# Where the scan's gate weights are split, who writes its reciprocals, and what its query parts are queued behind

## The chip, the cores and the metric

The kernel runs on one core of one Trainium2 chip. The metric is device time in microseconds (us) of one execution. The engines in the profile are PE (TensorE: matmuls, with PEld for its weight loads), DVE (VectorE), ACT (ScalarE), POOL (GpSimd) and SP (SyncE, which here only issues DMAs). Each engine works through its own queue in order.

## The reference

The program is one block of a latent generator with batch 1, 2048 latent tokens, 256 context tokens, width 1024 and depth 1: a gated linear recurrence (HGRN2, 8 heads of 128, both directions), then a gated convolutional feed-forward, both with RMS norm, shift, scale and gate. What matters here is the recurrence of one head and direction, in chunks:

```python
q, zf_fwd, zf_bwd, v, g = jnp.split(h @ w_in, 5, axis=-1)
f = lb[d] + (1.0 - lb[d]) * jax.nn.sigmoid(zf)      # forget gates, k = 1 - f
b = jnp.cumsum(jnp.log(f), axis=3)                  # within a chunk
scores = jnp.where(mask, (q * jnp.exp(b - b_ref)) @ (k * jnp.exp(b_ref - b)).T, 0.0)
kv = (k * jnp.exp(b_last - b)).T @ v                # a chunk's addition to the state
s = decay[..., None] * s + kv                       # from chunk to chunk
o = scores @ v + (q * jnp.exp(b)) @ s_start
```

Context tokens come first: the latent scans start from the states that they end in. The result of both directions is normalized per head, gated, multiplied by the output weights and added to the residual stream.

## The kernel before

All matmuls work on fp32 operands that are split in two parts (`split`, L79 to L82: ACT writes the high part at L80, DVE the rest at L81) and take three products each.

**The early stage** (`early`, L253 on) loads and normalizes the tokens and multiplies them by the weights of v, of the output gates and of q, by a scheme with seven products per block (`FACTORS`: B11, B21, T2, T1, T3, B22, T4). It goes once over the second half of the tokens (g = 1), then, from `turn_over` on, over the first half (g = 0), 84 products of four steps, each step three matmuls and one tick of a clock. Things beside the products are put on an agenda by tick (`at`). The generator `rest` is such a thing: `ada_rest` (L716) sums four rows of the modulation from 32 loads of `w_ada`, and `weights_rest` (L749) takes the two forget-gate weight matrices of each of the 8 heads, loads them raw (L757), splits them and stores both parts in DRAM (`w_d`, L766). Both work in one tile, `spare`, with the tag `cxt`: `weights_rest` uses two of its four rows for raw matrices and two for the result. 54 steps of `rest` are put on the agenda, five or six ticks apart; what is left of them is run out at the last T2 product of g = 0. Behind it the factor B12 is loaded again (`load_factor`, L782) into a tile with the same tag `cxt`, split, and put into the place that T2 held.

**The scan** (`mixer_scan`, L921) loads the split context tokens into a tile with that tag too (L1357) and goes over two groups of tokens (g = 0, 1) and over 8 heads in each. `head` (L1360) does, in group 0, the context's gates and states, and then for two units of four token tiles: `gate` (two projections of 48 matmuls' worth of work, L967 to L969, then sigmoid and bounds on ACT, L991 and L993) and `unit`. `weight` (L1344) loads the split forget-gate weights of the next head from `w_d`, or, for output gates, the raw ones through a buffer with two tiles (L1352).

`unit` calls `factors` (L1002), which scans the gates on DVE into prefix products `S` (L1011), forms `ke` from their differences, and lets GpSimd form the products of chunk totals (`TB`, `TX`, L1025 on). DVE takes the reciprocals of the 32 totals (`rt`, L1045), and GpSimd copies 15 of them into `d2` (L1046 and L1047), the second operand of the suffix scans (`suffix`, L1057). `rest` forms the query parts `qp` and `qi` and the key parts `km`, `kd` and part of `ke`. `unit_steps` has the matmuls behind it: `scores` (transposes L1100, scores L1144, mask on DVE L1161, sum `at` L1162), `stepped(p)` (products kv L1175, states on DVE L1178, copy `sk` on ACT L1181), and `outputs(p)` (L1196, L1199). The parts of a unit are put on the agenda at given ticks behind its gates, so that they fall among the gate matmuls of the next unit. A scheduler builds each engine's queue from the order in which instructions are traced and from when their inputs are ready by its own model; `tc.issue_after(i)` makes it put instructions behind `i` on that engine. `tied` (L1223) does so with the last entry of `made_last`, which `rest` and `scores` append to; it is used for the output weights that are scaled in the second group (L1243, L1249).

## Time and profile before

| what | us |
|---|---|
| median of 3 runs (2805.26 to 2810.89) | 2807.38 |
| profiled execution | 2804.56 |
| its span, first to last instruction | 2802.6 |
| early stage, to the last of its matmuls | 0 to 559.8 |
| scan | 612 to 1308 |
| output projection, up projection, down projection | 1308 to 2802 |

The span is shorter than the execution by 2.0 us, which lie around the instructions. Busy time is a union of an engine's instructions. A timeline row is: start, duration, engine, line, operation, output <- input, and in brackets how long the engine stood idle before it and what released it. A row of waits is: who waited, for whom, us in total, times, longest. SPq is SP's queue; its rows are issues of DMAs, not their transfers.

### The profile page before, as it was taken

What the parts mean: (1) busy time and instruction counts of PE and PEld (TensorE: products, weight loads), DVE (VectorE), ACT (ScalarE), POOL (GpSimd) and SP (SyncE); (2) the same over time, 40 slices, a digit from 0 to 9 for tenths busy, and PEclk for the clock granted to TensorE, in tenths of its full rate; (3) what the DMA queues carried; (4) which work ended last, traced back from release to release, by engine and by line L of the source; (5) the groups of instructions that cost most, each with busy time, mean ns of one, the idle gap of its engine ahead of it and who ended that gap; (6) DMA issues with size and microseconds to landing.
All of it is one profiled execution on the core that took longest, in us unless ns stands there. A gap on an engine that the chain in (4) does not pass through costs nothing.

```text
span 2802.6 us, 42181 instructions
## 1 busy us (share of the span) xinstructions
PE 2669.8 (95%) x15800; PEld 2219.7 (79%) x15800; DVE 2086.5 (74%) x2921; ACT 1191.1 (42%) x2051; POOL 610.4 (22%) x998
## 2 busy tenths in 40 slices
PE   7999999929999999999999999999999999999999
PEld 4788787828888777777888888888888888888887
DVE  4866876527777768786988888877878777577887
ACT  4744534412333222233666444444444444333444
POOL 1000333202222121121111443333444332000001
PEclk9999999969999999999999999999999999999999
DMA  8755766853343745445888522226322223888653
GB/s 325 278 194 203 244 211 204 288 218 114 93 132 119 247 134 192 151 130 191 288 300 324 209 91 90 88 70 237 134 89 91 91 72 113 293 294 282 208 191 128
DMA packets 260219, 514.90 MB, mean 184 GB/s; under 512 B 28448, under 2 KB 141488, under 8 KB 249392
## 3 DMA queue, kind: packets, MB, share of 16 engines
q1 hardware_dynamic: 255296, 502.98, 52.9%
q10 hardware_dynamic: 4720, 9.24, 0.9%
q8 instruction: 124, 2.03, 0.3%
q14 instruction: 79, 0.65, 0.1%
HBM read 352.48 MB, written 159.66 MB: 183 GB/s over the span
## 4 chain that ended last, share of the span: by engine, by line
PE 53%; DVE 3%; issue 1%; DMA 1%; ACT 1%; POOL 0%; POOLq 0%; DVEq 0%; ACTq 0%; SPq 0%
PE y L2096 5%; PE y L2095 5%; PE y L2097 5%; PE zc L1494 3%; PE zc L1496 3%; PE zc L1497 3%; PE zd L1497 3%; PE za L1497 3%; PE zd L1496 3%; PE za L1496 3%; PE zd L1494 3%; PE za L1494 3%; PE y L1598 2%; PE y L1600 2%; PE y L1599 2%; PE zb L1497 1%
## 5 line engine op out<-in xcount | busy, mean ns | idle before, releaser
L80 ACT ACTIVATE w<-raw 128x512 fp32r<-128x512 f32 (+1 forms) x270 | 169.2, 632 | 207.8 <-PE zd L1497 75.3
L81 DVE TENSOR_TENSOR w<-raw,w 128x512 fp32r<-128x512 f32 (+1 forms) x270 | 211.7, 788 | 50.8 <-ACT w L80 48.4
L2096 PE MATMUL y<-w,mh 128*128 128x512 f32 x600 | 233.5, 389 | 0.1
L2097 PE MATMUL y<-w,ml 128*128 128x512 f32 x600 | 233.4, 389 | 0.0
L2095 PE MATMUL y<-w,mh 128*128 128x512 f32 x600 | 233.2, 389 | 0.0
L81 DVE TENSOR_TENSOR w<-s,w 128x512 fp32r<-128x512 f32 x195 | 177.7, 915 | 71.4 <-ACT w L80 69.9
L80 ACT ACTIVATE w<-s 128x512 fp32r<-128x512 f32 x195 | 121.7, 630 | 199.6 <-POOL s L220 79.6
L1011 DVE TENSOR_TENSOR_SCAN S<-F,d 128x528 f32<-128x528 f32 (+1 forms) x80 | 91.4, 1143 | 103.1 <-ACT F L993 103.1
L76 POOL TENSOR_TENSOR rs<-rs,mhalf 128x1 f32<-128x1 f32 (+3 forms) x53 | 55.9, 1057 | 451.5 <-DVE rs L75 451.5
L967 PE MATMUL z<-tok,w 128*128 128x512 f32 x352 | 149.6, 425 | 0.0
L969 PE MATMUL z<-tok,w 128*128 128x512 f32 x352 | 141.5, 402 | 0.0
L968 PE MATMUL z<-tok,w 128*128 128x512 f32 x352 | 140.8, 400 | 0.0
L1494 PE MATMUL zc<-rT,w 128*128 128x512 f32 x352 | 137.1, 389 | 1.7 <-DMA rT<-rhs1T 1.7
L1496 PE MATMUL zc<-rT,w 128*128 128x512 f32 x352 | 137.0, 389 | 0.0
L1497 PE MATMUL zc<-rT,w 128*128 128x512 f32 x352 | 136.9, 389 | 0.0
L219 POOL TENSOR_TENSOR s<-raw 128x512 f32<-128x512 f32 x54 | 93.3, 1728 | 199.2 <-DMA raw<-in_w_up_dram 128.0
L2096 PEld LDWEIGHTS y<-w,mh 128*128 128x128 f32 x600 | 112.6, 188 | 23.7 <-DVE w L81 0.6
L2095 PEld LDWEIGHTS y<-w,mh 128*128 128x128 f32 x600 | 112.6, 188 | 23.7 <-ACT w L80 0.3
L2097 PEld LDWEIGHTS y<-w,ml 128*128 128x128 f32 x600 | 112.6, 188 | 23.5
L1496 PE MATMUL za<-rB,w 128*128 128x512 f32 x336 | 130.7, 389 | 0.0
L1497 PE MATMUL za<-rB,w 128*128 128x512 f32 x336 | 130.7, 389 | 0.0
L1494 PE MATMUL za<-rB,w 128*128 128x512 f32 x336 | 130.7, 389 | 0.0
(470 smaller groups left out, 7766.1 us busy)
## 6 DMA issues: line engine op xcount, KB each, us to landing
raw<-in_w_up_dram SPq DMA_DIRECT2D x88, 512.0 KB, 3.5
w<-w SPq DMA_DIRECT2D x32, 1024.0 KB, 8.2
raw<-in_w_in_dram SPq DMA_DIRECT2D x59, 512.0 KB, 4.6
lr<-m SPq DMA_DIRECT2D x49, 512.0 KB, 4.7
m<-r SPq DMA_DIRECT2D x66, 256.0 KB, 3.4
spare<-in_w_ada_dram SPq DMA_DIRECT2D x32, 512.0 KB, 4.8
w<-spare SPq DMA_DIRECT2D x16, 1024.0 KB, 4.9
kq<-stash SPq DMA_DIRECT2D x15, 1024.0 KB, 7.3
```

The source lines that it names most:

```text
L80: i = act.activation(h, src, AF.Copy)
L81: j = dve.tensor_tensor(l, src, h.bitcast(F32), OP.subtract)
L219: eng.tensor_tensor(s1, a21, a22, OP.add)
L967: pe.matmul(z, w[:, 0, k], h, start=k == 0, stop=False, skip_group_check=True)
L968: pe.matmul(z, w[:, 0, k], l, start=False, stop=False, skip_group_check=True)
L969: pe.matmul(z, w[:, 1, k], h, start=False, stop=k == KT - 1, skip_group_check=True)
L1494: pe.matmul(o, w[:, 0, k], r[:, :, 0, k], start=start and k == 0, stop=False, skip_group_check=True)
L1496: pe.matmul(o, w[:, 0, k], r[:, :, 1, k], start=False, stop=False, skip_group_check=True)
L1497: i = pe.matmul(o, w[:, 1, k], r[:, :, 0, k], start=False, stop=k == 3, skip_group_check=True)
L2095: pe.matmul(z, lh, rh, start=start, stop=False, skip_group_check=True)
L2096: pe.matmul(z, lh, rl, start=False, stop=False, skip_group_check=True)
L2097: pe.matmul(z, ll, rh, start=False, stop=stop, skip_group_check=True)
```

## The change

It has three parts. The forget-gate weights are no longer split by the early stage: `weights_rest` is gone, `rest` is `ada_rest` alone with 37 steps 7 ticks apart, and in the scan's first group `weight` loads the raw matrix, splits it and stores it to `w_d` for the second group. The reciprocals are written by DVE straight to where they are read: those of the suffix scans into `d2` (with one more chunk in it, for the scan's start value), the others into a smaller `rt`; the two copies on GpSimd are gone. And `rest` of a unit is tied behind the first two states of the unit before it: `made_last` is now appended to by `stepped(0)` alone. The last part of a unit moves from tick 30 to 31.

```diff
-        def weights_rest():
...
-            for n, (h, ty) in enumerate(todo):
-                load(n + 1)
-                w = hl.bitcast(F32R)
-                split(w[:, 0], w[:, 1], ring[:, n % 2])
-                sp.dma_start(w_d[h][ty - 1], hl.rearrange("p i n -> p (i n)"))
-                yield
...
-        rest = all_rest()
+        rest = ada_rest()
...
-                for m in range(54):
-                    at(clock[0] + 16 + 5 * m + m // 4, lambda: next(rest, None))
+                for m in range(37):
+                    at(clock[0] + 16 + 7 * m, lambda: next(rest, None))
...
-        d2 = fix.tile([128, 2, NS, SEG], F32, name="d2")
+        d2 = fix.tile([128, 2, NS + 1, SEG], F32, name="d2")
...
+            def strided(x, dist):
+                return bass.AP(tensor=x.tensor, offset=x.offset,
+                               ap=[list(x.ap[0]), [dist * SEG, 2], [2 * SEG, NS // 2]])
+
+            if u is not None:
+                dve.reciprocal(strided(d2[:, 0, 2, 0], NS), strided(S[:, 0, 1, 32], NS - 1))
+                rt = gp.tile([128, 2, NS // 2], F32, name="rt", tag="rt", bufs=2)
+                dve.reciprocal(rt, strided(S[:, 0, 0, 32], NS + 1))
...
-            rt = mid("rt", (2, NS))
-            dve.reciprocal(rt, S[:, :, :, 32])
-            pool.tensor_copy(d2[:, 0, 2:NS:2, 0], rt[:, 0, 1:NS - 1:2])
-            pool.tensor_copy(d2[:, 1, 1:NS:2, 0], rt[:, 1, 0:NS:2])
...
-                made_last.append(dve.tensor_tensor(halves(ke), halves(ke), halves(rt),
-                                                   OP.mult).ins)
+                c = ke[:, 0, 0, 0]
+                kh = bass.AP(tensor=c.tensor, offset=c.offset,
+                             ap=[list(c.ap[0]), [(NS + 1) * 32, 2], [64, NS // 2], [1, 32]])
+                scaled(kh, kh, rt)
...
-                made_last.append(dve.tensor_tensor(at_, AB[:, 0], AB[:, 1], OP.add).ins)
+                dve.tensor_tensor(at_, AB[:, 0], AB[:, 1], OP.add)
...
+                    moved = dve.scalar_tensor_tensor(st[s + 1], st[s], sd[:, 1, s:s + 1], kv[:, 1, i],
+                                                     OP.mult, OP.add).ins
+                if p == 0:
+                    made_last.append(moved)
...
-                if ty < 3:
+                if g and ty < 3:
                     sp.dma_start(flat, w_d[h][ty - 1])
                 else:
                     raw = rawp.tile([128, D], F32, name="raw", tag="raw")
                     sp.dma_start(raw, a["w_in"][h, ty])
                     split(w[:, 0], w[:, 1], raw.rearrange("p (k n) -> p k n", k=KT))
+                    if ty < 3:
+                        sp.dma_start(w_d[h][ty - 1], flat)
...
-                m, *parts = factors(h, u, t0[u], q, values(v_d[h][n]))
-                for f, dt in zip((*parts, *unit_steps(h, t0[u], m)), after):
+                m, suffix, rest = factors(h, u, t0[u], q, values(v_d[h][n]))
+                behind = (lambda: tied(rest)) if made_last else rest
+                for f, dt in zip((suffix, behind, *unit_steps(h, t0[u], m)), after):
                     at(clock[0] + dt, f)
```

## The prediction, made before the changed kernel was built or run

> **What bounds the kernel now.** I read the page first, for which engine the span is made of, then a table of stretches, then TensorE's own waits, then the timeline at the two places where it waits.

> ```profile
> span 2802.6 us, 42181 instructions
> PE   7999999929999999999999999999999999999999
> ...
> 450.00:559.50 109.50, 106.81 (x474) 86.74 (x472) 65.79 (x85) 47.89 (x76) 32.18 (x33) 1.00 0.74 253
> 559.50:612.00 52.50, 0.31 (x2) 0.00 (x0) 10.19 (x12) 7.66 (x11) 2.19 (x6) 0.53 0.79 296
> 612.00:634.00 22.00, 21.87 (x115) 19.67 (x116) 6.14 (x11) 6.76 (x11) 2.83 (x9) 0.88 0.02 7
> 634.00:948.00 314.00, 305.35 (x3047) 265.01 (x3046) 235.89 (x350) 94.78 (x187) 73.48 (x259) 1.00 0.43 133
> 948.00:1227.00 279.00, 257.93 (x2600) 218.05 (x2603) 208.90 (x291) 76.29 (x143) 50.52 (x197) 0.96 0.52 164
> 1227.00:1308.00 81.00, 75.22 (x766) 63.41 (x754) 60.18 (x97) 31.76 (x72) 13.16 (x45) 0.98 0.39 120
> ```

> The columns behind a stretch are its length, busy time of PE, PEld, DVE, ACT and POOL, granted clock, DMA share and GB/s. TensorE fills the span but for one slice, the ninth, and that slice is the hole 559.5 to 612.0 between the early products and the scan. In the scan's first group of heads (634 to 948) PE is idle 8.7 us in 314, in its second (948 to 1227) 21.1 us in 279, and there the granted clock is 0.96 too. DVE is at 75% in both. So time comes from holes in PE's queue, and no other engine is a bound of its own.

> PE's waits, for 450 to 559, 558.9 to 612.6, 634 to 948 and 948 to 1227:

> ```profile
> PE za L517 <- ACT u L546: 1.5, 2, 1.0
> ...
> 612.13 0.55 PE L967 MATMUL z<-cxt,w 128*128 128x256 f32 x1 [52.32 <-DMA cxt<-cxt]
> ...
> PE kv L1175 <- ACT sk L1181: 4.3, 7, 0.6
> PE o L1199 <- DVE at L1162: 2.9, 7, 1.6
> PE o L1196 <- DVE states L1178: 1.5, 7, 0.3
> ...
> PE kv L1175 <- ACT sk L1181: 10.6, 14, 1.1
> PE o L1196 <- DVE states L1178: 10.5, 14, 1.0
> ```

> **Part 1, the weights that leave the early stage.** What ended last in the hole, on SP, ACT, DVE and PE:

> ```profile
> 584.13 0.32 SPq L766 DMA_DIRECT2D w<-spare  x1
> 591.45 0.32 SPq L766 DMA_DIRECT2D w<-spare  x1
> 595.39 0.57 SPq L782 DMA_DIRECT2D fraw<-part  x1
> 604.03 0.33 SPq L1357 DMA_DIRECT2D cxt<-cxt  x1
> ...
> 589.11 1.06 ACT L80 ACTIVATE spare<-spare 128x1024 fp32r<-128x1024 f32 x1 [6.26 <-DMA w<-spare]
> 600.85 2.19 ACT L80 ACTIVATE tok<-fraw 128x512 fp32r<-128x512 f32 x4 [10.68 <-DMA fraw<-part]
> ...
> 590.20 1.22 DVE L81 TENSOR_TENSOR spare<-spare 128x1024 fp32r<-128x1024 f32 x1 [6.09 <-ACT spare L80]
> ...
> 559.42 0.39 PE L520 MATMUL zc<-rT,w 128*128 128x512 f32 x1
> ```

> The 16 weight matrices go through one output buffer: ACT stands until the previous store has landed, so one costs 7.3 us (584.13 to 591.45), and the chain of 16 outruns the products by 32 us. The tile is then needed twice more: for factor B12 (load at 595.39, in at 600.85, split until 604.03) and for the context tokens (load at 604.03, first matmul at 612.13). That is 3.9 us from the last store to the load, 5.5, 3.2 and 8.1 us.

> Removed from the early stage: 16 loads, 16 ACT (1.06 us), 16 DVE (1.22 us), 16 stores. Then the tile is free when the 37 steps of the ada sums are through, due at tick 16 + 7 x 36 = 268 of 336 from the turn-over. A tick is three matmuls, and 474 matmuls in 109.5 us are 0.231 us each, so the tile comes free about 68 x 0.69 = 47 us before 559.5, near 513. B12's load lands near 519. Its splits must wait for the end of the last T2 product, whose place B12 takes: 8 products of 12 matmuls, 22 us, before the end, 537. With 3.2 us of splitting and 8.1 us of load the context tokens are in near 549, 10 us before PE asks for them. The first scan weights now need raw loads and splits first:

> ```profile
> 525.75 0.38 SPq L1352 DMA_DIRECT2D raw<-in_w_in_dram  x1
> ...
> 542.19 0.33 SPq L1352 DMA_DIRECT2D raw<-in_w_in_dram  x1
> ```

> These two loads are for gate weights of the last head, used after 1227: SP sends a load as soon as its buffer is free, and both raw buffers are free by 542. The new loads take those slots, so two splits (2 x 1.22 us on DVE) fit ahead of 559.5. I take 1 us for what is left of the hole: **52.3 - 1 = 51.3 us** saved. The hole also leaves the clock low: 0.88 over 22 us is **2.6 us**, gone with it. Early PE waits for ACT's u, which stands behind the split that waits for its store, 1.5 us in two, go as well.

> In the scan's first group the same 16 splits are added, less 16 loads of 1 MB, and 16 stores and 16 raw loads more on SP. DVE gets 16 x 1.22 = 19.5 us in 314 us (75% to 81%), ACT 17 us on 30%. Behind a split on ACT stand the gates' sigmoids, behind it on DVE the scans, and PE waits for both; behind a store on SP stand loads of q and v. Bounds: 0 if they fall in idle time, 16 x (1.06 + 1.22) = 36 us if each holds PE for its whole length. I take the near end, because a quarter of DVE's time and two thirds of ACT's are idle there and PE has three gate banks, but book only half of what this group could gain (below).

> **Part 2, reciprocals and the order behind the states.** One unit of the second group, DVE, then PE:

> ```profile
> 968.84 0.35 DVE L1045 RECIPROCAL rt<-S 128x32 f32<-128x32 f32 x1
> 970.67 1.32 DVE L1057 TENSOR_TENSOR_SCAN S<-F,rt,d 128x528 f32<-128x528 f32 x1 [1.48 <-POOL d L1046]
> 973.05 1.29 DVE L1161 COPY_PREDICATED AB<-mbf,sc 128x1024 f32<-128x1024 uint32 x1
> 974.22 0.69 DVE L1063 TENSOR_TENSOR qp<-q,S 128x512 f32<-128x512 f32 x1
> 974.82 0.69 DVE L1162 TENSOR_TENSOR at<-AB 128x512 f32<-128x512 f32 x1
> 975.42 0.69 DVE L1064 TENSOR_TENSOR qp<-q,S 128x512 f32<-128x512 f32 x1
> 976.02 0.35 DVE L1178 SCALAR_TENSOR_TENSOR states<-Sf,sd,kv 128x128 f32<-128x128 f32 x1
> 977.42 0.35 DVE L1178 SCALAR_TENSOR_TENSOR states<-states,sd,kv 128x128 f32<-128x128 f32 x1
> ...
> 975.35 0.38 PE L1196 MATMUL o<-Sf,qi 128*128 128x128 f32 x2
> 976.42 0.49 PE L1196 MATMUL o<-states,qi 128*128 128x128 f32 x2 [0.37 <-DVE states L1178]
> 978.24 1.16 PE L1175 MATMUL kv<-v,kt 128*128 128x128 f32 x8 [1.10 <-ACT sk L1181]
> ```

> The suffix scan waits 1.48 us for GpSimd's copies of the reciprocals. With VectorE writing them itself nothing is left between: the suffix scans start 1.48 us sooner, less the second reciprocal. The trace has none of 16 elements; the nearest row is the 32-element one, 0.35 us, so two cost 0 to 0.35 us more than one; I take 0.2 and gain 1.3 us. Then the query parts: ahead of the second state stand qp twice (0.6 us apart each) and qi, which fills 976.3 to 977.4, 1.1 us: 2.3 us that the tie moves behind it. The second state then ends near 977.8 - 1.3 - 2.3 = 974.2 (its two states, 0.35 us each, back to back), ACT's copy at 974.6, before PE reaches its first output matmul at 975.35. Both waits of the unit go, with 0.7 us to spare. The tie adds a wait to the query parts; behind them on DVE stand km, kd and the next prefix scan, and PE's next transposes wait for kd. But states now end 3.6 us sooner, so the moved 2.3 us end sooner than they did.

> The second group's PE waits are 10.6 + 10.5 = 21.1 us in 14 units. Idle time counts from a matmul's modelled end, and one lasts 0.39 us (the row at 559.42) where they follow each other every 0.231, so each wait hides 0.16 us of lost overlap more: 28 x 0.16 = 4.5 us, together **26 us**. The clock:

> ```profile
> 1014.00:1020.00 6.00, 4.53 (x19) 3.80 (x19) 6.00 (x11) 1.36 (x3) 1.20 (x2) 0.73 0.71 173
> 1093.00:1099.00 6.00, 4.47 (x27) 3.68 (x26) 6.00 (x11) 1.96 (x4) 0.00 (x0) 1.00 0.39 134
> ```

> 0.96 over 279 us is 11.2 us. The 6 us with 1.5 us of idle PE at 1014 run at 0.73; the 6 us with the same idle at 1093 at full clock. I take it that the low clock comes from the idle time, in some of the units, and goes with it: **11 us**; the other end is 0.

> [...]

> First group: 4.3 + 2.9 + 1.5 = 8.7 us in 21 waits, 12 us with the lost overlap. Half of it, because of the splits: **6 us**. The last head and all behind the scan I leave as they are.

> **Sum:** 51.3 + 2.6 + 1.5 + 26 + 11 + 6 = 98.4 us. The profiled execution took 2804.6 us (2.0 around its span of 2802.6) and would take 2706.2; the median of the runs is 2.8 us above it, so **2709 us**. This case alone goes from 2694 (the hole's last 1 us, the other 6 of the first group, 5.8 of PE idle and 1.6 of clock in the last head) to 2718.

> **Rivals.**

> A, the chain to the context tokens is late: SP takes its queue in order, and the last store of the products is this:

> ```profile
> 562.19 0.51 SPq L529 DMA_DIRECT2D q<-out  x1
> ```

> If the context load goes behind it, it lands at 562.7 + 8.1 = 570.8, 11 us of hole; if B12's load and splits go there as well, 16.8 us and more. 10 to 16 us lost and some clock: 2722. For it: four early stores hold SP in turn. Against: loads were sent ahead of such stores in the rows above.

> B, another step of DVE takes the states' place, or the query parts aren't what held them: part 2 gives nothing in PE time, 26 + 11 + 6 = 43 us, 2752; half of it 2730. Against: a spare of 0.7 us and DVE at 75%.

> [...]

> D, the splits hold PE in the first group: up to 36 + 6 us, 2751; half 2730.

> E, slower than before. ACT takes its queue in order, and each split stands at its head until its raw transfer is in, as in the row at 589.11. If PE pays the early stage's whole 7.3 us cycle for each of 16, that is 117 us, and the first group's 6 aren't won: 2709 + 6 + 117 = 2832. It decides from 5.8 us a split on ((98.4 - 6) / 16). Against it: two raw buffers and loads a head ahead; PE has three gate banks. [...]

> **Chances.** Forecast 0.62, A 0.13, B 0.09, C 0.08, D 0.05, E 0.03. The range is 2691 (the near end, 2694, less the 2.8 us between runs) to 2736 (A, C and the halves of B and D are in; E and the ends of B and D are out). Faster than before by over 0.2% (5.6 us, about what a measurement of this kernel can tell from no change) is all but E and a point for mishaps between: 0.96; within it 0.01; slower 0.03.

> **What would show it.** PE's wait for the context tokens under 3 us; no split or store of the spare tile in the early stage; both reciprocals directly ahead of the suffix scans, with no wait for GpSimd; the states ahead of qp; the second group's unit period at 17 us instead of 19 and its clock at 1.00; in the first group no wait on a split's DMA. I would be wrong by a hole of 10 us or more near 560, by PE waits for states that stay, or by waits of the gates behind the splits.

## The result and the profile after

| | before | after |
|---|---|---|
| median, us | 2809.14 (4 runs, 2805.26 to 2811.89) | 2705.41 (4 runs, 2701.87 to 2707.88) |
| profiled execution, us | 2804.56 | 2705.35 |
| its span, us | 2802.6 | 2703.5 |

The ratio is 0.9631 (95% interval 0.9614 to 0.9648): 103.7 us less. The span lost 99.1 us, and three points in both traces say where. They are the scan's first matmul (612.1 us before, 556.2 after), the second prefix scan of the 16th unit (947.9 us before, 888.4 after) and that of the 30th unit (1227.1 and 1128.0); the 14 units between the last two stand for the second group.

| stretch, us | before | after | less |
|---|---|---|---|
| early stage, to its last matmul's end (after: to the scan's first matmul, which starts ahead of that end) | 559.8 | 556.2 | 3.6 |
| hole between it and the scan | 52.3 | 0 | 52.3 |
| first group, from the scan's first matmul | 335.8 | 332.2 | 3.6 |
| second group, 14 units | 279.2 | 239.6 | 39.6 |
| all behind it | 1575.5 | 1575.5 | 0 |

The table of stretches after, with columns as before, from the scan's start on:

```profile
556.30:577.00 20.70, 20.36 (x119) 17.73 (x118) 10.57 (x17) 9.37 (x14) 5.10 (x15) 1.00 0.85 312
577.00:888.40 311.40, 303.88 (x3044) 264.98 (x3043) 248.82 (x376) 105.55 (x198) 70.97 (x229) 0.99 0.47 154
888.40:1128.00 239.60, 238.91 (x2609) 206.38 (x2611) 211.08 (x305) 73.69 (x144) 43.69 (x169) 1.00 0.58 189
```

The scan's start has full clock (0.88 before). In the second group PE is idle 0.7 us in 239.6 (21.1 in 279 before), and its clock is 1.00. In the first group it is idle 7.5 us in 311 (8.7 in 314 before). One stretch of that group, from 601.1 to 604.5, runs at half clock (0.50), which costs 1.7 us by estimate (half of 3.41) and is why its row says 0.99.

The way to the scan, after: SP's queue, then ScalarE's and VectorE's, then TensorE's:

```profile
513.20 0.58 SPq L758 DMA_DIRECT2D fraw<-part  x1
...
539.71 0.32 SPq L1336 DMA_DIRECT2D cxt<-cxt  x1
...
535.25 2.18 ACT L80 ACTIVATE tok<-fraw 128x512 fp32r<-128x512 f32 x4
...
539.00 0.68 DVE L81 TENSOR_TENSOR tok<-fraw,tok 128x512 fp32r<-128x512 f32 x1
...
555.99 0.39 PE L520 MATMUL zc<-rT,w 128*128 128x512 f32 x1
556.22 0.28 PE L943 MATMUL z<-cxt,w 128*128 128x256 f32 x1
```

B12's load goes out at 513.20, its last split ends at 539.7, and the load of the context tokens stands right behind it at 539.71. With the 8.1 us that it took before, it is in at 547.8, 8 us early. The scan's first matmul starts 0.23 us behind the start of the last product.

PE's waits after, first for the first group from 577, then for the second:

```profile
PE o L1173 <- DVE states L1153: 4.4, 7, 0.8
...
PE kv L1150 <- ACT sk L1158: 0.6, 1, 0.6
...
PE o L1176 <- DVE at L1137: 0.3, 1, 0.3
```

The second group's 28 waits are down to one of 0.3 us. In the first group the waits for `sk` went (4.3 to 0.6 us), and waits for states came in their place (1.5 to 4.4); the line left out is one wait of 1.8 us for `at`.

One unit of the second group after, on VectorE, then on GpSimd:

```profile
922.19 1.26 DVE L987 TENSOR_TENSOR_SCAN S<-F,d 128x528 f32<-128x528 f32 x1 [1.52 <-ACT F L969]
923.48 0.26 DVE L998 RECIPROCAL d<-S 128x16 f32<-128x16 f32 x1
923.65 0.20 DVE L1000 RECIPROCAL rt<-S 128x16 f32<-128x16 f32 x1
923.77 0.63 DVE L1003 TENSOR_TENSOR ke<-S 128x512 f32<-128x512 f32 x1
925.50 2.47 DVE L1037 TENSOR_TENSOR_SCAN S<-F,d 128x528 f32<-128x528 f32 x2 [1.10 <-POOL sd L1012]
...
930.19 0.35 DVE L1153 SCALAR_TENSOR_TENSOR states<-states,sd,kv 128x128 f32<-128x128 f32 x1
930.46 0.68 DVE L1044 TENSOR_TENSOR qp<-q,S 128x512 f32<-128x512 f32 x1
...
923.78 0.66 POOL L1028 COPY TX<-S 128x4 f32<-128x4 f32 x1
```

Two things are to be seen. The states (the second is shown) stand ahead of `qp`, as the tie wants it. And the suffix scan still waits 1.10 us for GpSimd, though both reciprocals are VectorE's own: it writes over `S`, and GpSimd's chain of products (L1009 to L1015, L1028 to L1031) still reads the chunk totals out of `S`. The scan starts 2.05 us behind the end of the prefix scan (923.45 to 925.50); it was 2.48 before (968.19 to 970.67).

### The profile page after: what moved, and what is told of

Same layout as the page of the kernel before. It is cut to its first block, busy times and chain, and to the rows that moved or that the text cites. A ratio compares the mean times of both kernels' runs of the same rounds, so it can differ in the third digit from the quotient of the medians.

```text
span 2703.5 us, 42065 instructions
## 1 busy us (share of the span) xinstructions
PE 2646.1 (98%) x15800; PEld 2205.9 (82%) x15800; DVE 2074.4 (77%) x2953; ACT 1187.3 (44%) x2051; POOL 597.9 (22%) x934
## 4 chain that ended last, share of the span: by engine, by line
PE 72%; DVE 10%; DMA 3%; POOL 1%; ACT 1%; issue 1%; SPq 0%; POOLq 0%; DVEq 0%; ACTq 0%
PE y L2076 4%; PE y L2075 4%; PE y L2077 4%; PE z L943 3%; PE z L945 3%; PE z L944 3%; PE zc L1474 3%; PE zc L1476 3%; PE zc L1477 3%; PE zd L1476 3%; PE za L1476 3%; PE za L1477 3%; PE zd L1477 3%; PE zd L1474 3%; PE za L1474 3%; PE y L1580 2%
## 5 line engine op out<-in xcount | busy, mean ns | idle before, releaser
L80 ACT ACTIVATE w<-raw 128x512 fp32r<-128x512 f32 (+1 forms) x286 | 186.1, 656 | 215.9 <-PE zd L1477 75.0
L81 DVE TENSOR_TENSOR w<-raw,w 128x512 fp32r<-128x512 f32 (+1 forms) x286 | 226.8, 797 | 64.3 <-ACT w L80 61.8
L81 DVE TENSOR_TENSOR w<-s,w 128x512 fp32r<-128x512 f32 x195 | 173.0, 892 | 81.8 <-ACT w L80 80.2
L80 ACT ACTIVATE w<-s 128x512 fp32r<-128x512 f32 x195 | 121.7, 630 | 204.8 <-POOL s L220 82.5
L943 PE MATMUL z<-tok,w 128*128 128x512 f32 x352 | 145.6, 414 | 0.0
L945 PE MATMUL z<-tok,w 128*128 128x512 f32 x352 | 138.5, 394 | 0.0
L944 PE MATMUL z<-tok,w 128*128 128x512 f32 x352 | 138.0, 392 | 0.0
L1158 ACT ACTIVATE sk<-kv 128x256 f32<-128x256 f32 x64 | 24.6, 384 | 256.4 <-DVE states L1153 121.1
L2077 PEld LDWEIGHTS y<-w,ml 128*128 128x128 f32 x600 | 112.6, 188 | 23.6
```

Source lines behind the costliest of these rows:

```text
L80: i = act.activation(h, src, AF.Copy)
L81: j = dve.tensor_tensor(l, src, h.bitcast(F32), OP.subtract)
L943: pe.matmul(z, w[:, 0, k], h, start=k == 0, stop=False, skip_group_check=True)
L944: pe.matmul(z, w[:, 0, k], l, start=False, stop=False, skip_group_check=True)
L945: pe.matmul(z, w[:, 1, k], h, start=False, stop=k == KT - 1, skip_group_check=True)
L2077: pe.matmul(z, ll, rh, start=False, stop=stop, skip_group_check=True)
```

## The experiments

Theory at this point: the tie brings the second group's gain, the reciprocals little, because GpSimd's reads of the totals hold the suffix scans instead. Rivals: the reciprocals bring it; or the first part does, by way of an earlier or less disturbed scan. Twelve kernels ran. The ratios are against runs of the kernel before on the same chip, whose medians were 2807.97, 2812.08, 2810.75 and 2810.71 us in the four groups of runs (E1 to E4, E5 to E8, E9 to E11, E12).

| kernel | us | ratio (95% interval) | first group | second group | a unit at full clock | stretches at clock 0.5 there |
|---|---|---|---|---|---|---|
| before | 2809.14 | 1 | 335.8 | 279.2 | 19.0 | 7 |
| E1 first part alone | 2747.53 | 0.9785 (0.9771 to 0.9800) | 330.8 | 277.5 | 19.0 | 6 |
| E2 and reciprocals | 2750.38 | 0.9799 (0.9782 to 0.9815) | 335.7 | 278.7 | 18.6, later 19.8 | 5 |
| E3 first part and tie | 2712.57 | 0.9661 (0.9647 to 0.9676) | 332.9 | 245.4 | 17.3 | 0 |
| after, all three | 2705.41 | 0.9631 (0.9614 to 0.9648) | 332.2 | 239.6 | 16.9 | 0 |
| E4 all, totals copied | 2692.05 | 0.9588 (0.9573 to 0.9602) | 324.1 | 237.4 | 16.9 | 0 |
| E5 as E4, no tie | 2715.63 | 0.9656 (0.9640 to 0.9671) | 328.2 | 256.8 | 17.6, later 18.8 | 0 |

The stages are from the profiled executions, cut as above; a unit's length is the distance of its second prefix scan from the next unit's.

### E1: the first part alone

The reciprocals, their copies on GpSimd, `made_last` and tick 30 are those of before; the early stage and `weight` are those of after.

```diff
-                dve.reciprocal(strided(d2[:, 0, 2, 0], NS), strided(S[:, 0, 1, 32], NS - 1))
...
+            rt = mid("rt", (2, NS))
+            dve.reciprocal(rt, S[:, :, :, 32])
+            pool.tensor_copy(d2[:, 0, 2:NS:2, 0], rt[:, 0, 1:NS - 1:2])
+            pool.tensor_copy(d2[:, 1, 1:NS:2, 0], rt[:, 1, 0:NS:2])
...
-                behind = (lambda: tied(rest)) if made_last else rest
+                behind = rest
```

> The first part alone: the weights leave the early stage, reciprocals and order as before. If the parts add up as the prediction has them: no wait for the context tokens, early stage some 3 us shorter, the scan's second group as before (279 us for 14 units, 21 us of PE waits, clock near 0.96), so 57 us less than before, about 2750 us. If the splits hold PE in the first group (rival D): up to 36 us more, 2750 to 2786, with PE waits behind the gates there.

2747.53 us, 60.4 less than before. PE's waits in its first group, then in its second:

```profile
PE o L1172 <- DVE states L1154: 4.2, 8, 0.9
PE kv L1151 <- ACT sk L1157: 2.4, 7, 0.6
...
PE kv L1151 <- ACT sk L1157: 10.6, 14, 1.1
PE o L1172 <- DVE states L1154: 10.5, 14, 1.0
```

The second group's waits are those of before to the tenth, so the first part does nothing there. And the 16 splits cost the first group nothing that can be seen in its sum: 330.8 us, where before it took 335.8 with 2.6 of low clock in it, and no wait of PE names a split or a gate behind one. The waits moved, though: those for `sk` fell from 4.3 to 2.4 us, those for states rose from 1.5 to 4.2.

### E2: the first part and the reciprocals, without the tie

```diff
-                    moved = dve.scalar_tensor_tensor(st[s + 1], st[s], sd[:, 1, s:s + 1], kv[:, 1, i],
-                                                     OP.mult, OP.add).ins
-                if p == 0:
-                    made_last.append(moved)
+                    dve.scalar_tensor_tensor(st[s + 1], st[s], sd[:, 1, s:s + 1], kv[:, 1, i],
+                                             OP.mult, OP.add)
...
-                behind = (lambda: tied(rest)) if made_last else rest
+                behind = rest
```

> First part and reciprocals on VectorE, query parts not tied. The prediction's step (nothing left between the reciprocals and the suffix scans, 1.3 us sooner): the waits for states go and those for sk shrink to half, 15 to 20 us and some clock less than the weights alone, about 2730 us. Rival from the trace of the changed kernel: the suffix scan overwrites the totals that GpSimd still reads, so it starts only 0.4 us sooner and still waits some 1 us for GpSimd in each unit; the second group gains at most 6 us, about 2744 us.

2750.38 us, no faster than E1 (the intervals overlap). The view of VectorE's queue in one of its later units shows why the second group gained nothing:

```profile
1051.18 2.47 DVE L1037 TENSOR_TENSOR_SCAN S<-F,d 128x528 f32<-128x528 f32 x2 [1.09 <-POOL sd L1012]
...
1056.55 1.28 DVE L1225 SCALAR_TENSOR_TENSOR spare<-spare,vec,g 128x1024 f32<-128x1024 f32 x1
...
1058.01 1.21 DVE L1052 TENSOR_TENSOR qi<-qp,TB 128x1024 f32<-128x1024 f32 x1
1059.14 0.34 DVE L1154 SCALAR_TENSOR_TENSOR states<-states,sd,kv 128x128 f32<-128x128 f32 x1
```

GpSimd holds the suffix scan for 1.09 us, so units became 0.4 us shorter (19.0 to 18.6), the 0.43 us by which the scan starts sooner. And from the sixth unit on, the scaled output weights (L1225) and `qi` both stand ahead of the second state, 1.2 us more, where in E1 from there on `qi` stood behind it. Nothing in the edit asks for that; the scheduler's order came out another way. So a queue that is left to the scheduler can take back what a faster instruction gives. The first group took 4.9 us more than E1's, with 3.7 us more of idle PE; what held it there was not looked into.

### E3: the first part and the tie, reciprocals copied by GpSimd

The edit is that part of E1's which concerns the reciprocals; the tie and tick 31 stay.

> First part and the tie, reciprocals copied by GpSimd as before. By the prediction's numbers the tie gives 2.3 us of the 2.9 that are needed, so 0.6 us a unit stay: 8 us and some clock above the whole change, about 2715 us. Rival: the tie does nearly all of it, second group without waits for states or sk, within 3 us of the whole change, 2705 to 2708 us.

2712.57 us, 35.0 less than E1. The second group falls from 277.5 to 245.4 us, with one wait of 0.6 us left on PE, and no stretch at half clock, though VectorE waits 21.9 us for GpSimd. PE's waits there, then PE in one unit:

```profile
PE o L1176 <- DVE at L1137: 0.6, 1, 0.6
```

```profile
935.80 0.39 PE L1176 MATMUL o<-v,at 128*128 128x128 f32 x2
936.21 0.49 PE L1173 MATMUL o<-states,qi 128*128 128x128 f32 x2
```

The tie does nearly the whole work; the reciprocals bring what is left, from 0.9661 to 0.9631, 7 to 8 us. The table of waits hides where that lies: units take 17.30 us, and 16.87 with the reciprocals. The matmul that reads the third state starts 0.41 us behind the pair ahead of it, 0.22 in the whole change; the state ends at 936.15. A delay that is shorter than the modelled end of the matmul ahead (0.39 us) isn't shown as idle time.

### E4: the whole change, with the totals copied for GpSimd

VectorE copies the 32 totals to a tile of their own, from which GpSimd reads them:

```diff
+            tt = gp.tile([128, 2, ns], F32, name="tt", tag="tt", bufs=1)
+            dve.tensor_copy(tt, S[:, :, :, 32])
+            tot = tt.rearrange("p d (s g) -> p d s g", g=4)
...
-            tot = S[:, :, :, 32].rearrange("p d (s g) -> p d s g", g=4)
```

> The whole change, and VectorE copies the 32 totals to a tile of their own from which GpSimd works, so that the suffix scan overwrites nothing that GpSimd reads. If GpSimd's reads of the totals are what the suffix scans wait for now: those waits (31 us in all) are gone, the suffix starts about 1 us sooner, and the waits for states in the first group (4.4 us) go with them, 3 to 6 us less than the whole change, about 2701 us. If the splits hold the states there: the suffix waits go, the PE waits stay, 2705 us.

2692.05 us: faster than the change itself, by 13 us between the medians and 12 by the ratios. VectorE's queue in one unit, then PE's wait for states in the first group:

```profile
912.36 1.26 DVE L987 TENSOR_TENSOR_SCAN S<-F,d 128x528 f32<-128x528 f32 x1 [2.54 <-ACT F L969]
913.72 0.19 DVE L998 COPY tt<-S 128x32 f32<-128x32 f32 x1
...
914.65 2.45 DVE L1039 TENSOR_TENSOR_SCAN S<-F,d 128x528 f32<-128x528 f32 x2
```

```profile
PE o L1175 <- DVE states L1155: 2.1, 6, 0.4
```

The suffix scan follows the prefix scan by 1.03 us (913.62 to 914.65), with no wait in the row: 1.45 us sooner than before the change, for a copy of 0.19 us. In the first group this takes 8.1 us off (1.7 of them the stretch at half clock), in the second 2.2. Behind it the traces differ by 3.5, which can't be told from scatter: that part takes from 1571.5 to 1580.7 us in the traces of these kernels. So the hold by GpSimd is shown: take it away, and the time goes.

### E5: E4 without the tie

> The first part, the reciprocals on VectorE and the copy of the totals, but not the tie. In the run with the first part and the reciprocals alone (2750.4 us) the suffix scans of the second group still waited 15.2 us for GpSimd, which was reading totals out of the tile that they overwrite, and TensorE waited 15.6 us for sk and 7.7 us for states. If that hold is what kept the prediction's 1.3 us from coming, the suffix scans now start at once behind the reciprocals, about 1 us sooner a unit, and the states with them. Theory one, the order behind the states is needed too: qp, qp and qi still stand between the first and the second state, 2.3 us, so of 23 us of waits about 8 to 10 stay, the clock stays low in part, and the time is 2725 to 2738 us. Rival, as the prediction's sum of steps would have it if 1.3 us were enough: the waits go as with the tie, and the time is 2695 to 2705 us. Second rival, the suffix scans gain nothing for the states, because something else on VectorE stands ahead of them: 2745 us or more.

The edit is E2's on top of E4's. 2715.63 us, between what the two main theories gave, and far from the third. Units of the second group take 17.6 us, 1.4 less than E1's, then 18.8 from the sixth on, where the scaled output weights and `qi` stand ahead of the second state as in E2. PE still waits 13.5 us in 22 waits; E4 has none, and is faster by 23.6 us between the medians and 19 by the ratios: the tie is needed too, but less is lost without it than was expected. What the expectation had too high is the clock: E5's second group has 13.5 us of waits and not one stretch at half clock, where E2 with 23.3 us has five. E12 takes that up.

### E6, E7, E8: what E4 still waits for

E6 moves the first outputs of the last head, E7 makes the key parts an item of their own, tied behind the next states; E8 does both.

```diff
-                        at(c + 44 + 10 * i, lambda hs=hs: top_outputs(hs))
+                        at(c + 48 + 12 * i, lambda hs=hs: top_outputs(hs))
...
-                if p == 0:
-                    made_last.append(moved)
+                (made_next if p else made_last).append(moved)
...
+                behind = (lambda: (tied(rest), tied(keys, made_next))) if made_last else \
+                    (lambda: (rest(), keys()))
```

> The whole change, the copy of the totals, and the four steps of the last head's first outputs issued 4 to 6 steps later in its list. In the run with the copied totals (2692.05 us) TensorE waits 3.6 us (2 waits, 2.7 us of idle time) in the last head for ScalarE's oi, which holds a PSUM buffer of o. Theory: the wait is one of place only, nothing behind it is late, and it goes: about 2689 us, 2.5 to 3.5 us less. Rival: the first outputs' later place makes the normalisation at the end later by as much: 2692 us, no difference, with a new wait near the end. Second rival: slower, 2694 to 2698, if the outputs now hold the last units' matmuls.

> The whole change, the copy of the totals, and in the first group the key parts (km, kd) as an item of their own, tied behind the next states of the other direction. In the run with the copied totals the first group's outputs still wait 2.1 us for states in 6 waits, and in the whole change 4.4 us in 7: the states of the second direction stand behind qi, the context scans, km and kd there. Theory: those waits go, 2 to 4 us with the lost overlap: 2688 to 2690 us. Rival: kd comes later, and TensorE's next transposes of the keys wait for it, about 0.5 to 1 us in each of 15 units: 2697 to 2707 us.

> The two changes of order together, with the whole change and the copy of the totals. If each does what its own theory says, they lie in different stages and add up: 2685 to 2688 us. If the keys come too late, the loss of that run less 3 us: 2694 to 2704 us. If neither moves anything: 2692 us.

2691.17, 2692.36 and 2691.28 us; the ratios 0.9566 (0.9551 to 0.9582), 0.9572 (0.9554 to 0.9590) and 0.9568 (0.9548 to 0.9587) can't be told from E4's. In the last head, E4's PE waits 3.6 us for `oi` (L1274). In E6 it waits 1.0 us for that and 1.0 us for `so`, 1.6 us less, but all that lies behind the second group takes 1572.8 us instead of 1572.0: no gain can be seen, as the first rival had it.

In E7 PE's waits for states in the first group are 1.7 us in 6 instead of 2.1 in 6, and the group takes 324.0 us instead of 324.1. The unit's key parts did move behind the third state, but in five of the six places something else took their place:

```profile
645.60 0.69 DVE L1023 TENSOR_TENSOR kd<-ke,TB 128x512 f32<-128x512 f32 x1 [0.85 <-POOL TB L1017]
646.21 0.34 DVE L1158 SCALAR_TENSOR_TENSOR states<-states,sd,kv 128x128 f32<-128x128 f32 x1
```

The `kd` of 512 columns is the context's. VectorE stands idle 0.85 us for GpSimd's `TB` ahead of it, with the state behind it in the queue; in E4 it stood behind the states.

### E9, E10, E11: a delay ahead of the suffix scans

A copy of part of `S` onto itself, of 256 numbers a partition (E9) or 512 (E10, E11), ahead of each suffix scan of the second group; E9 and E10 on top of E5, E11 on top of E4.

```diff
             def suffix():
+                if late:
+                    dve.tensor_copy(S[:, 0, 0:16, 1:SEG], S[:, 0, 0:16, 1:SEG])
```

> The run without the tie (2715.63 us: the first part, the reciprocals, the copied totals), with one VectorE copy of 128x256 numbers onto themselves ahead of each suffix scan of the second group. It holds the states later by its length, somewhere between 0.19 us (the 128x32 copy) and 0.69 us (a 128x512 instruction with two inputs); estimate 0.3 us. In the run without it TensorE's waits for sk and states add up to 1.35 us at most in any of the 3.41 us stretches after which the clock may change, and none of the scan's stretches is at half clock. In the runs with low clocks, stretches of 3.41 us with 1.47 us or more of idle time were followed by one at half clock, those with 1.43 us or less were not. Theory, the clock goes by the idle share of a stretch, with a limit near 1.5 us: with 1.35 + 0.3 us, 2 to 7 stretches fall to 0.5, each costs about 1.7 us, and the time is 2722 to 2732 us. [...]

> The same with a copy of 128x512 numbers, estimate 0.5 us. Theory, a limit near 1.5 us of idle time in 3.41 us: 6 to 9 stretches at half clock in the second group, 2715.6 + 14 x 0.5 + 6 to 9 x 1.7 = 2733 to 2738 us. Rival, only the delays count: 2721 to 2724 us.

> The best kernel so far (the whole change and the copied totals, 2692.05 us) with the same 128x512 copy ahead of each suffix scan of the second group. In the second group of that kernel TensorE waits for nothing. Theory, the states end ahead of TensorE's need by the 0.7 us that the prediction worked out, and by 0.4 us more with the totals copied: a delay of 0.5 us is hidden, 2690 to 2694 us, with no wait for sk or states in the second group. Rival, there is no such spare time and the delay shows in each of 14 units: 2698 us or more, with waits for sk of 0.3 us and more.

E9 and E10 took 2710.16 and 2711.64 us (ratios 0.9649, 0.9628 to 0.9670, and 0.9655, 0.9631 to 0.9679), no slower than E5, against the theory in both and against E10's rival: as a test of the clock they failed. The reason is in E10's queue:

```profile
1019.29 0.34 DVE L1158 SCALAR_TENSOR_TENSOR states<-states,sd,kv 128x128 f32<-128x128 f32 x1
1019.54 1.21 DVE L1056 TENSOR_TENSOR qi<-qp,TB 128x1024 f32<-128x1024 f32 x1
```

With one more instruction the scheduler put the second state ahead of `qi` by itself. PE's idle time in the second group is 8.6 us, and 13.5 in E5. So more work on VectorE made no slower kernel, since the order came out better, which is E2's finding from the other side.

E11 took 2696.77 us (0.9599, 0.9572 to 0.9625; not to be told from E4's 0.9588). Its median is 2.8 us above the range that was expected, but its second group takes 237.4 us, to the tenth that of E4, and PE waits for nothing there. What it has more lies ahead of the scan and behind the group: its scan began at 559.9 us, E4's at 554.6. The copy took 0.43 us, and that much is to spare ahead of the states.

### E12: a later `sk`, with the other queues as they were

E5 with ScalarE's copy `sk` made twice in the second group ahead of the last head; the order of TensorE's, VectorE's and GpSimd's queues is E5's.

```diff
-                act.activation(sk, kv[:, 0], AF.Copy)
+                [act.activation(sk, kv[:, 0], AF.Copy) for _ in range(m["copies"])]
...
-                m, suffix, rest = factors(h, u, t0[u], q, values(v_d[h][n]))
+                m, suffix, rest = factors(h, u, t0[u], q, values(v_d[h][n])); m["copies"] = 2 if g and not last else 1
```

> The run without the tie (2715.63 us) with ScalarE's copy sk made twice in the second group's 14 units ahead of the last head; the queues of TensorE, VectorE and GpSimd keep their order, which the two late copies on VectorE did not leave as it was. The copies of sk are 0.28 us apart in the trace, so TensorE's wait for sk grows from 1.10 to about 1.38 us, and the idle time of a 3.41 us stretch that holds both waits of a unit from 1.35 to about 1.63 us. Theory, the clock goes by the idle share of a stretch with a limit near 1.5 us: a third of the units have both waits in one stretch, 2 to 6 stretches of the second group fall to 0.5, about 1.7 us each, and with 14 x 0.28 = 4 us of delay the time is 2723 to 2730 us. [...]

2731.38 us (0.9712, 0.9684 to 0.9741), 1.4 us above the theory's range. PE's waits for `sk` grew from 11.5 to 18.7 us, more than the 4 us foreseen, and three stretches of the second group run at half clock, where E5 had none. Stretches of 3.41 us of E12, in pairs, each with the one behind it (columns as above; the first times are length and PE's busy time, and the clock is the third number from the end):

```profile
1062.46:1065.87 3.41, 1.65 (x11) 1.25 (x10) 3.41 (x7) 1.34 (x4) 0.00 (x0) 1.00 0.71 258
1065.87:1069.28 3.41, 3.41 (x13) 2.95 (x12) 3.41 (x6) 0.42 (x2) 0.00 (x0) 0.50 0.43 107
966.88:970.29 3.41, 1.77 (x15) 1.54 (x14) 3.41 (x7) 1.63 (x4) 0.00 (x0) 1.00 0.57 180
970.29:973.70 3.41, 3.41 (x21) 2.92 (x20) 3.41 (x6) 0.12 (x1) 0.00 (x0) 1.00 0.68 208
```

PE is busy all through the second stretch of each pair. Behind 1.76 us of idle time (3.41 - 1.65) it runs at half clock, with 13 instructions instead of 21; behind 1.64 us it does not.

## Why the prediction was right, point by point

| term | predicted, us | measured, us |
|---|---|---|
| the hole | 51.3 | 52.3 |
| low clock at the scan's start | 2.6 | 2.6 (0.88 before, 1.00 after) |
| early waits | 1.5 | 3.6 |
| second group: waits and overlap 26, clock 11 | 37 | 39.6 |
| first group | 6 | 1.0 (3.6 less the 2.6 above) |
| all behind it | 0 | 0 |
| sum | 98.4 | 99.1 |

That the sum comes out within 1 us is luck: a term too large and three too small cancel. And one step of part 2, what the reciprocals gain, was wrong; the term held because another figure, when TensorE needs the states, was off the other way.

**The hole: right by its own steps.** B12's load was put near 513 (513.20), its splits near 537 (535.25 to 539.7), the context tokens in near 549 (547.8, by the load's time of before). Rival A, SP late past its stores, did not come.

**The early stage.** Its waits for `u` are gone, 1.5 us. The other 2.1 us can't be told from scatter: in the 13 kernels that share this early stage, the scan's first matmul starts anywhere from 554.4 to 559.9 us.

**The reciprocals: this step failed.** "With VectorE writing them itself nothing is left between: the suffix scans start 1.48 us sooner, less the second reciprocal." They start 0.43 us sooner. GpSimd's queue in that unit of before shows why:

```profile
968.26 0.72 POOL L1025 COPY TB<-S 128x8 f32<-128x8 f32 x1 [5.15 <-DVE S L1011]
...
970.03 0.22 POOL L1028 TENSOR_TENSOR sd<-TB,S 128x8 f32<-128x8 f32 x1
...
970.44 0.20 POOL L1046 COPY d<-rt 128x7 f32<-128x7 f32 x1
970.57 0.20 POOL L1047 COPY d<-rt 128x8 f32<-128x8 f32 x1
```

The copies were the last 0.3 us of a queue of twelve; nine instructions ahead of them read `S`, until 970.25, and the suffix scan must wait for those as well. The row on VectorE named only the last of them. Where the hold is gone too (E4) the scans start 1.45 us sooner, and units without the tie shrink by 1.4 (E5): the 1.3 was the right size for a step that the change does not make. The price, 0.2 us more for two reciprocals than for one, was near: 0.26 and 0.20 us in the trace against 0.35, and the second begins 0.17 us behind the first.

**The tie: right, and it carried the step that failed.** It was to move 2.3 us behind the second state, and E3 shows that it alone takes all but 0.6 us of the waits that the view shows. What it moved was read off one unit: `qi` stands ahead of the second state in 5 of before's 14 units. In the other 9 the scaled output weights (L1249, or L1243 once) stand there, some 1.2 us as well, and they moved too, since they are tied by the same list `made_last`. No run takes these two ties, or the move from tick 30 to 31, apart.

The 0.7 us to spare weren't there as they were worked out. ScalarE's copy was to end 0.75 us ahead of the first output matmul. After, that matmul starts at 930.58 in the unit shown, the second state ends at 930.54, and the copy only follows:

```profile
930.62 0.39 ACT L1158 ACTIVATE sk<-kv 128x256 f32<-128x256 f32 x1 [4.95 <-DVE states L1153]
...
931.47 1.06 PE L1150 MATMUL kv<-v,kt 128*128 128x128 f32 x8
```

But the matmul that needs the copy is not the first output's; it is this one, 0.89 us behind it. The copy ends at 931.01, 0.46 us ahead. So the prediction set TensorE's need 0.89 us too early, and that made up for the 0.87 us (1.3 less 0.43) that the reciprocals failed to bring. That both waits went was right; that they went with this sum was luck.

The wait that the tie adds to `qp` and `qi` hides, as forecast. Rival B, another step of VectorE in the states' place, was half there: that step exists (GpSimd's hold), but with the tie it ends early enough in the second group.

**The second group's size.** At full clock a unit went from 19.0 to 16.87 us; 14 x 2.13 = 29.8 us stands against 26, so by estimate the lost overlap of a wait was 0.3 us rather than 0.16 ((29.8 - 21.1) / 28). Before's 14 units took 13.2 us more than 14 x 19.0; its seven stretches at half clock account for 12.0 of that (7 x 1.71), against 11. After's 14 units take 3.4 us more than 14 x 16.87, at full clock: one of 17.6 us and the group's last two of 18.1 and 18.2.

**The clock: right.** The prediction's two stretches of before, whose equal idle time had given 0.73 and 1.00, are told apart by where the idle time lies:

```profile
1013.30:1016.71 3.41, 1.94 (x13) 1.49 (x13) 3.41 (x8) 0.91 (x2) 0.00 (x0) 1.00 0.37 102
1016.71:1020.12 3.41, 3.41 (x13) 2.93 (x12) 3.41 (x5) 0.45 (x2) 1.32 (x2) 0.50 0.90 217
1095.20:1098.61 3.41, 2.04 (x14) 1.80 (x15) 3.41 (x8) 1.36 (x3) 0.00 (x0) 1.00 0.57 195
1098.61:1102.02 3.41, 3.41 (x21) 2.94 (x20) 3.41 (x7) 0.00 (x0) 0.85 (x2) 1.00 1.03 298
```

1.47 us idle inside one stretch of the clock's own grid (3.413 us in these traces), and the next runs at half clock; 1.37 us, and it doesn't. The border isn't sharp: the stretches of before at 975.8 and 1074.7 have 1.47 and 1.49 us idle, and the next ones keep full clock, against what E9's expectation read from the traces. Short waits do lower the clock here, and it comes back with them gone: the second group's clock is 0.96 with 21.1 us of them before, 1.00 with 0.3 us after, and longer waits for `sk` alone (11.5 us in E5, 18.7 in E12) brought three stretches of half clock where there was none.

**The first group: the reason was wrong, and the size.** Half of 12 us was booked "because of the splits", and 1.0 us came. E1 shows that the splits cost the group nothing in sum, and rivals D and E fall with it. One place is an exception: after the change two splits (588.32, 2.35 us) stand on VectorE ahead of a prefix scan whose gates were ready at 588.1. PE then waits 1.8 us for `at` at 598.2 and 0.4 us for states, and the stretch at half clock follows at 601.1. That the splits are the cause there is likely, and no run tests it. Elsewhere what keeps the waits is VectorE's queue. Who VectorE waits for there, after (one row of six), and a place where PE waits 0.76 us:

```profile
DVE S L1037 <- POOL sd L1012: 14.7, 15, 1.1
```

```profile
687.82 1.20 DVE L1052 TENSOR_TENSOR qi<-qp,TB 128x1024 f32<-128x1024 f32 x1
...
690.54 1.22 DVE L1021 TENSOR_TENSOR kd<-ke,TB 128x1024 f32<-128x1024 f32 x1
691.67 0.34 DVE L1153 SCALAR_TENSOR_TENSOR states<-states,sd,kv 128x128 f32<-128x128 f32 x1
...
692.07 0.49 PE L1173 MATMUL o<-states,qi 128*128 128x128 f32 x2 [0.76 <-DVE states L1153]
```

GpSimd holds the suffix scans for 14.7 us in 15 units, ScalarE waits for a raw transfer of a split just once (0.9 us), and the third state stands behind `qi` and `kd` (and what lies between them). With the hold gone (E4) the group takes 11.7 us less than before, 9.1 without the low clock, of the 12 that were thought possible.

## What to carry to other kernels

When a wait names one releaser, look at what else the waiting instruction writes over and who still reads it: here GpSimd, which reads a few numbers out of a large tile, held the tile's next writer for 1.10 us in the unit shown, and a copy of 0.19 us freed it. Where a scheduler orders a queue, the order is worth more than any one instruction's length: a tie that names what must come first gained 35 us by itself, and an edit without it can lose its gain to a new order. Short waits of the matmul engine cost more than their length here, in lost overlap and in clock: 21.1 us of them in the second group of before stand against 29.8 us in its units at full clock and, by estimate, 12.0 us of half clock.

## What the runs showed of the hardware

| idle in the stretch, us | stretches | followed by half clock |
|---|---|---|
| under 1.20 | 10521 | 0 |
| 1.20 to 1.46 | 46 | 1 |
| 1.46 to 1.60 | 35 | 16 |
| 1.60 to 1.77 | 21 | 5 |
| over 1.77 | 58 | 58 |

Between 1.46 and 1.77 us half clock followed 21 of 56 stretches, so the modelled idle time alone doesn't decide there; what else does was not settled. Half clock for one stretch of 3.41 us costs, by estimate, up to 1.7 us (half of it), about as much again as the idle time that brings it.

**GpSimd beside VectorE's scans.** In E4 GpSimd's copies of four numbers run while the suffix scans do, which start at 914.65 and take 2.45 us for two:

```profile
914.72 1.22 POOL L1030 COPY TX<-tt 128x4 f32<-128x4 f32 x1
...
917.04 0.20 POOL L1032 TENSOR_TENSOR TX<-tt 128x4 f32<-128x4 f32 x1
```

This one and the next (1.21 us from 915.88) take as long as one scan each, and the first instruction behind both scans 0.20 us. What made them as long as that was not shown. The chain that held the suffix scans after the change has such a copy too: the one at 923.78 took 0.66 us beside a VectorE instruction of 0.63, where it took 0.19 in the unit of before, at 969.04.
